# Layer A's projections by one level of Strassen's scheme, with pooled input, gate and residual kept in memory

## The chip, the cores and the metric

The kernel runs on one core of a Trainium2 chip. The metric is device time in microseconds (us); before the change the median of three runs is 2950.09 us. Engine names follow the profile: PE multiplies matrices (PEld is its weight load), DVE, ACT and POOL work elementwise, SP issues most of the DMAs. Each engine works through its own list of instructions in a fixed order; an instruction that waits holds up everything behind it on that engine.

## The reference

One step of a streaming encoder: one layer A, a shared projection to keys and values, one layer B with attention. 512 prompt positions and 8 streams of 16 new positions are worked on together: 640 columns. The change lies in layer A:

```
h = rmsnorm(x, norm_a)                        # x: 640 rows of 2048
z = h @ w_in_a                                # 2048 -> 2 * 4096
u, gate = z[..., :4096], z[..., 4096:]
# four groups g of 1024 channels, trailing windows w = 2, 4, 8, 16 along the stream
d = (windowed sum of u over w) / count - u
y = concat(d_g @ w_grp_a[g]) * scale          # 1024 -> 1024 for each group
x = x + (y * silu(gate)) @ w_out_a            # 4096 -> 2048
state = the last 15 rows of u, an output
```

After it come `hk = rmsnorm(x, norm_kv)`, `hk @ w_kv` (K, V and forget logits), layer B and the last norm. All data is float32. A product is made of three passes: each operand is split in a high part (float32r) and the rest, and high*high, high*rest and rest*high are summed.

## The kernel before

The stream lies in SBUF turned, features on partitions: `xh`, `xl` hold the two parts of the normed-by-weight input (16 k-tiles of 128 features, 640 columns), `acc` the residual. A weight tile is the stationary operand (128x128), and 320 columns of the stream pass through it; `mm3` issues the three passes for both halves, six matmuls, for a k-tile and a block of 128 outputs.

`gemm_pair` makes a pair of blocks (256 outputs). For every two k-tiles it loads 128x512 weights (`raw`), ACT writes the high part `whi`, DVE the rest `wlo`. Layer A runs by group: four `u_pair` (16 k-tiles each), then four times `gate_pair` (16 k-tiles) and `y_pair` (8 k-tiles, from the pooled input `d8`, which stays in SBUF), and `out_pairs`, the output projection over four k-tiles at a time, added to `acc` by DVE. An output bank of PSUM is one of three, so one pair can be emptied while the next is made.

`u_pair` also does the windowed sums: g + 1 additions of 774 columns for each block, on DVE (L348), then the difference `dd`. At the end of layer A `after(k)` splits each finished k-tile of `acc` and sums its squares on POOL (L473), beside the last output projections; `norm_stream` makes the row factor `R` from the sums, and `proj` starts K.

PE's order is the program's (`manual_schedule`); the order on the other engines is set by a scheduler when the kernel is built.

```
def mm3(acc_, wh, wl, xh, xl, first, last):
    for w, x, f, l in ((wh, xh, first, False), (wh, xl, False, False), (wl, xh, False, last)):
        for s in range(2):
            nc.tensor.matmul(acc_[:, s, :HALF], w, x[:, s * HALF : (s + 1) * HALF], start=f, stop=l)
```

Of the kernel before, what the change touches and what calls it, by code (L numbers as in the profile page):

```python
# [39 lines left out]
def tile_yoco_step(ctx, tc, i, o):  # L40
# [5 lines left out]
    big = ctx.enter_context(tc.tile_pool(name="big", bufs=1))  # L46
    wp = ctx.enter_context(tc.tile_pool(name="wp", bufs=1))
# [22 lines left out]
    R = const.tile([P, NT], F32, name="R")  # L70

    ps = ctx.enter_context(tc.tile_pool(name="ps", bufs=1, space=PSUM))
# [6 lines left out]

    def wchunk(src, nk, nn, scale=None, pin=False):  # L80
        raw = wp.tile([P, nk, nn], F32, tag="raw", name="raw", bufs=4)
        dma(raw, src)
        if scale is not None:
            nc.vector.tensor_tensor(raw, raw, scale.unsqueeze(2).to_broadcast([P, nk, nn]), op=ALU.mult)
        hi = wp.tile([P, nk, nn], F32R, tag="whi", name="whi", bufs=3)
        lo = wp.tile([P, nk, nn], F32R, tag="wlo", name="wlo", bufs=3)
        split(hi, lo, raw, pin)
        return hi, lo

    def mm3(acc_, wh, wl, xh, xl, first, last):  # L90
        for w, x, f, l in ((wh, xh, first, False), (wh, xl, False, False), (wl, xh, False, last)):
            for s in range(2):
                nc.tensor.matmul(acc_[:, s, :HALF], w, x[:, s * HALF : (s + 1) * HALF], start=f, stop=l)  # L93
# [18 lines left out]

    def tbank():
        return ps.tile([P, 512], F32, tag="t", name="tb", bufs=2)

    def transpose(out, x, n=P):
        nc.tensor.transpose(out, x, ident[:n, :n])  # L117
# [54 lines left out]
    win = i["w_in_a"][0].rearrange("(kt p) n -> p kt n", p=P)  # L172
    wkv = i["w_kv"].rearrange("(kt p) n -> p kt n", p=P)
    winb = i["w_in_b"][0].rearrange("(kt p) n -> p kt n", p=P)
    woutb = i["w_out_b"][0].rearrange("(kt p) n -> p kt n", p=P)
    wout = i["w_out_a"][0].rearrange("(kt p) n -> p kt n", p=P)

# [14 lines left out]

    xh = big.tile([P, KT, NT], F32R, tag="xh", name="xh")
# [4 lines left out]
    ordered = ctx.enter_context(ExitStack())  # L198
    ordered.enter_context(tc.manual_schedule(engines={mybir.EngineType.PE}))
    with tc.tile_pool(name="pa", bufs=1) as pa, tc.tile_pool(name="psa", bufs=1, space=PSUM) as psa:  # L200
        count = [0]

        def psmm():
            count[0] += 1
            if count[0] % 3 == 0:
                return psa.tile([P, 2, 512], F32, tag="mmx", name="mmx")
            return ps.tile([P, 2, 512], F32, tag="mm", name="mm", bufs=2)

        def load_rows(names, c0):
            rows = pa.tile([96, P], F32, tag="s0", name="rows")  # L210
            r0 = 0
            for nm in names:
                v = i[nm] if len(i[nm].shape) == 1 else i[nm][0]
                n = v.shape[0] // P
                dma(rows[r0 : r0 + n, :], v.rearrange("(r c) -> r c", c=P))
                r0 += n
            pc = tbank()
            transpose(pc[:, :r0], rows[:r0, :], r0)
            nc.vector.tensor_copy(cols[:, c0 : c0 + r0], pc[:, :r0])

        xq = [pa.tile([P, 4, TT, 256], F32, tag=t, name="xq") for t in ("dh", "dl")]
        ssq = pa.tile([P, TT, 2], F32, tag="mh", name="ssq", bufs=2)

        # the array's clock is raised once the array is busy: it is kept busy from the start
        idle = pa.tile([P, P], F32, tag="s1", name="idle")
        nc.vector.memset(idle, 0.0)
        warm = psa.tile([P, 2, 512], F32, tag="mmx", name="warm")
        for _ in range(8):
            nc.tensor.matmul(warm[:, 0, :P], idle, idle, start=True, stop=True)

        def load_eighth(e):
            x = xq[e // 4][:, e % 4]
            cs = slice(e * 256, (e + 1) * 256)
            if e == 0:
                load_rows(("norm_a",), 0)
            dma(x[:, 4, :], i["x_sample"].rearrange("b s d -> (b s) d")[:, cs])
            dma(x[:, :4, :], i["x_prompt"][0].rearrange("(t p) d -> p t d", p=P)[:, :, cs])

        def turn_eighth(e):
            x = xq[e // 4][:, e % 4]  # L240
            ks = slice(2 * e, 2 * e + 2)
            tp = ps.tile([P, 2, P], F32, tag="t", name="tp", bufs=2)
            for j in range(2):
                transpose(tp[:, j, :], x[:, 4, j * P : (j + 1) * P])
            xg = pa.tile([P, 2, P], F32, tag="tmp", name="xg")
            nc.vector.tensor_tensor(xg, tp, na_c[:, ks].unsqueeze(2).to_broadcast([P, 2, P]), op=ALU.mult)
            split(xh[:, ks, NP:], xl[:, ks, NP:], xg)
            nc.scalar.activation(acc[:, ks, NP:], tp, AF.Copy)
# [60 lines left out]
        def xs(k):  # L309
            return xh[:, k, :], xl[:, k, :]  # L310
# [697 lines left out]
```

## Time and profile before

| what | value |
|---|---|
| runs | 2948.26, 2950.09, 2950.49 us |
| profiled execution, first to last instruction | 2944.0 us |
| around it, against the median | 6.1 us |
| PE busy | 2921.5 us (99%) |
| DVE busy | 1457.7 us (50%) |
| ACT busy | 847.9 us (29%) |
| POOL busy | 34.7 us (1%) |
| layer A, to its last matmul | 1608 us |

How to read it: layer A takes a little over half of the span, and PE is busy throughout; the other engines have idle time. A busy PE is not a PE at its peak, since matmuls overlap, so the pace is read from the time between starts. Busy times of neighbouring DVE instructions overlap too: a 128x512 subtraction is listed with 0.68 us, and the next instruction starts 0.61 us after it.

### The profile page before, as it was taken

Reading aid. Unit: us, or ns where it says so; the run is one execution under the profiler, and the core shown is the slowest. Engines: PE = TensorE matmul, PEld = TensorE weight load, DVE = VectorE, ACT = ScalarE, POOL = GpSimd, SP = SyncE. Lnnn points to the kernel's source line nnn. Section 1 sums busy time; section 2 is a strip of 40 time slices with the busy share of each in tenths; the row PEclk is TensorE's granted clock in tenths of the full one; section 3 lists DMA queues with packets and bytes.
Section 4 is the critical chain, followed back from the end, with each engine's and each line's share of the span. In section 5 each row is a group of like instructions: output and inputs, shape, how many; then the busy total and the mean of one; then the engine's idle time right before and its main releaser. Section 6 shows DMA issues by size and latency. Waiting matters only on the chain.

```text
span 2944.0 us, 47606 instructions
## 1 busy us (share of the span) xinstructions
PE 2921.5 (99%) x19573; PEld 2828.4 (96%) x19573; DVE 1457.7 (50%) x2587; ACT 847.9 (29%) x1560; POOL 34.7 (1%) x73
## 2 busy tenths in 40 slices
PE   9999999999999999999999999999999999999998
PEld 9999999999999999999999899999999999999786
DVE  6423344333445333554337755655656666556434
ACT  5222222221222212222224232333333333334222
POOL 0000000000000000000003000000000000000000
PEclk9999999999999999999999999999999999999999
DMA  4222222222222222222224655455554555554822
GB/s 149 81 78 76 76 79 78 81 75 76 79 77 83 75 76 76 79 80 78 76 76 140 132 122 119 112 119 123 134 119 114 119 120 121 118 119 108 145 86 108
DMA packets 610282, 293.04 MB, mean 100 GB/s; under 512 B 281024, under 2 KB 595712, under 8 KB 609936
## 3 DMA queue, kind: packets, MB, share of 16 engines
q1 hardware_dynamic: 610064, 290.00, 38.5%
q8 instruction: 153, 2.51, 0.4%
q14 instruction: 65, 0.53, 0.1%
HBM read 261.28 MB, written 28.64 MB: 98 GB/s over the span
## 4 chain that ended last, share of the span: by engine, by line
PE 93%; DMA 2%; DVE 2%; SPq 1%; ACT 1%; issue 1%; DVEq 0%; POOL 0%; POOLq 0%; ACTq 0%
PE mm L93 35%; PE mmb L93 29%; PE mmx L93 17%; PE mmf L900 4%; PE po L832 2%; PE tb L117 1%; PE f L900 1%; PE ss L733 1%; DMA xt<-xres 1%; SPq L938 1%; DVE yn L941 0%; DMA raw<-in_w_in_b 0%; PE sp L743 0%; PE op L845 0%; PE op L844 0%
## 5 line engine op out<-in xcount | busy, mean ns | idle before, releaser
L78 DVE TENSOR_TENSOR wlo<-raw,whi 128x512 fp32r<-128x512 f32 x480 | 337.6, 704 | 793.6 <-ACT whi L75 791.4
L75 ACT ACTIVATE whi<-raw 128x512 fp32r<-128x512 f32 x480 | 302.7, 631 | 1012.2 <-PE mm L93 588.8
L93 PE MATMUL mmb<-xh,whi 128*128 128x320 f32 x2048 | 483.1, 317 | 2.6 <-DVE acc L413 2.6
L93 PE MATMUL mmb<-xh,wlo 128*128 128x320 f32 x2048 | 467.1, 309 | 0.0
L93 PE MATMUL mmb<-xl,whi 128*128 128x320 f32 x2048 | 466.9, 309 | 0.0
L93 PEld LDWEIGHTS mmb<-xh,whi 128*128 128x128 f32 x2048 | 337.1, 189 | 8.9 <-issue 6.5
L93 PEld LDWEIGHTS mmb<-xh,wlo 128*128 128x128 f32 x2048 | 342.9, 188 | 0.0
L93 PEld LDWEIGHTS mmb<-xl,whi 128*128 128x128 f32 x2048 | 342.8, 188 | 0.0
L93 PE MATMUL mm<-xh,whi 128*128 128x320 f32 x1408 | 325.8, 313 | 1.3 <-ACT xh L258 1.3
L93 PE MATMUL mm<-xl,whi 128*128 128x320 f32 x1408 | 321.7, 310 | 0.3 <-DVE xl L259 0.2
L93 PE MATMUL mm<-xh,wlo 128*128 128x320 f32 x1408 | 321.3, 309 | 0.0
L142 DVE TENSOR_TENSOR wlo<-raw,whi 128x512 fp32r<-128x512 f32 x272 | 188.3, 693 | 204.5 <-ACT whi L140 200.4
L140 ACT ACTIVATE whi<-raw 128x512 fp32r<-128x512 f32 x272 | 171.6, 632 | 377.4 <-PE mmb L93 232.1
L93 PEld LDWEIGHTS mm<-xl,whi 128*128 128x128 f32 x1408 | 235.6, 188 | 1.4 <-DVE xl L259 1.3
L93 PEld LDWEIGHTS mm<-xh,wlo 128*128 128x128 f32 x1408 | 235.8, 188 | 0.0
L93 PEld LDWEIGHTS mm<-xh,whi 128*128 128x128 f32 x1408 | 234.0, 188 | 1.8 <-ACT xh L258 1.5
L131 DVE TENSOR_TENSOR raw<-raw,cols 128x512 f32<-128x512 f32 x256 | 169.3, 676 | 4.8 <-DMA raw<-in_w_kv 2.2
L93 PE MATMUL mm<-mh,whi 128*128 128x320 f32 x688 | 157.4, 310 | 0.4 <-ACT whi L75 0.4
L93 PE MATMUL mm<-mh,wlo 128*128 128x320 f32 x688 | 156.7, 309 | 0.0
L93 PE MATMUL mm<-ml,whi 128*128 128x320 f32 x688 | 156.4, 308 | 0.0
L93 PE MATMUL mmx<-xh,whi 128*128 128x320 f32 x640 | 147.2, 311 | 0.0
L93 PE MATMUL mmx<-xh,wlo 128*128 128x320 f32 x640 | 145.8, 309 | 0.0
(306 smaller groups left out, 4187.9 us busy)
## 6 DMA issues: line engine op xcount, KB each, us to landing
raw<-in_w_in_a SPq DMA_DIRECT2D x256, 256.0 KB, 2.7
raw<-in_w_out_a SPq DMA_DIRECT2D x128, 256.0 KB, 2.8
raw<-in_w_kv SPq DMA_DIRECT2D x128, 256.0 KB, 3.0
raw<-in_w_in_b SPq DMA_DIRECT2D x128, 256.0 KB, 3.0
raw<-in_w_grp_a SPq DMA_DIRECT2D x64, 256.0 KB, 2.7
kc<-in_cache_k SPq DMA_DIRECT2D x64, 256.0 KB, 4.8
vc<-in_cache_v SPq DMA_DIRECT2D x16, 1024.0 KB, 7.6
raw<-in_w_out_b SPq DMA_DIRECT2D x64, 256.0 KB, 3.0
```

The source lines that it names most:

```text
L75: a = nc.scalar.activation(hi, x, AF.Copy)
L78: nc.vector.tensor_tensor(lo, x, hi.bitcast(F32), op=ALU.subtract)
L93: nc.tensor.matmul(acc_[:, s, :HALF], w, x[:, s * HALF : (s + 1) * HALF], start=f, stop=l)
L117: nc.tensor.transpose(out, x, ident[:n, :n])
L131: nc.vector.tensor_tensor(r, r, raws[n][1].unsqueeze(2).to_broadcast([P, 4, P]), op=ALU.mult)
L140: nc.scalar.activation(hi, raw, AF.Copy)
L142: nc.vector.tensor_tensor(lo, raw, hi.bitcast(F32), op=ALU.subtract)
L733: nc.tensor.matmul(sp[rows, b % 2 * PAST : (b % 2 + 1) * PAST], qs[:, rows], kct[:, b * PAST : (b + 1) * PAST], start=True, stop=True)
L832: nc.tensor.matmul(po[32 * q : 32 * q + 32, :P], pts[:, j, 32 * q : 32 * q + 32], vc[:, 4 * q + j, :], start=(j == 0), stop=False)
L900: nc.tensor.matmul(out, (ol if q == 2 else oh)[:, k, ts], wl if q == 1 else wh, start=first and q == 0, stop=last and q == 2)
L938: dma(xt[at].rearrange("p t (j r) -> p t j r", r=32), xres[n * 512 : (n + 1) * 512].rearrange("(j c) (t a r) -> a c t j r", c=32, a=4, r=3 ...
```

## The change

Layer A is written anew; K, V, layer B and the end keep their code. The matrix products of layer A go by blocks of 2x2: two k-tiles, two blocks of outputs, two halves of 320 columns. Seven products of block combinations take the place of eight products of blocks:

- `prep` makes, for two such pairs of k-tiles, the four combinations of the weights (three DVE instructions), then splits all seven operands at once (128x1792, ACT and DVE). Two buffers hold the outcome (`wh`, `wl`).
- `tbuild` makes the same for the stream side: four sums of 128x320, then split.
- `pair` runs one unit of 256 outputs: for each pair of k-tiles 7 x 3 matmuls into seven PSUM banks `m1` to `m7`, one buffer each. `combine` turns the seven banks into the four blocks (one copy on ACT, seven instructions on DVE).
- Phases: first the whole input is loaded, normed, turned and built into operands `kps` (`p0`); the turned residual goes to memory (`xacc`). Then 32 units, u and gate in turn, with the pooled input stored to memory (`dscr`) and the gate too (`gscr`). Then by group four `y_pair` and eight `out_pair`, whose outcome is added to `xacc` by an accumulating DMA from POOL's queue. At the end `acc` is loaded from `xacc`, and all 16 k-tiles are split and squared there.
- The windowed additions, and half of the sums for `kps`, go from DVE to POOL.
- Pools of later stages wait by tile.

The heart of the diff, cut:

```
+    PROD = (("m1", 1, 1), ("m6", 6, 6), ("m5", 3, 4), ("m7", 2, 5), ("m2", 5, 3), ("m3", 7, 2), ("m4", 4, 7))
...
+        def prep():
+            if raws:
+                w8 = raws.pop(0)
+                nc.vector.tensor_tensor(w8[:, :, 2:4, :], w8[:, :, 1:5:3, :], w8[:, :, 0:1, :].to_broadcast([P, 2, 2, P]),
+                                        op=ALU.subtract)
+                nc.vector.tensor_tensor(w8[:, :, 6, :], w8[:, :, 3, :], w8[:, :, 1, :], op=ALU.add)
+                nc.vector.tensor_tensor(w8[:, :, 7, :], w8[:, :, 6, :], w8[:, :, 5, :], op=ALU.subtract)
+                wh = wa.tile([P, 2, 7, P], F32R, tag="wh", name="wh", bufs=2)
+                wl = wa.tile([P, 2, 7, P], F32R, tag="wl", name="wl", bufs=2)
+                split(wh, wl, w8[:, :, 1:, :])
...
+        def pair(kps, hook=None):
+            pp = {m: psa.tile([P, 512], F32, tag=m, name=m)[:, :HALF] for m, _, _ in PROD}
+            for s in range(len(kps) // 2):
+                wh, wl = parts.pop(0)
+                prep()
+                fetch()
+                for kk in range(2):
+                    kp = 2 * s + kk
+                    h, l = kps[kp]
+                    for m, a, b in PROD:
+                        for q, (w, x) in enumerate(((wh, h), (wh, l), (wl, h))):
+                            nc.tensor.matmul(pp[m], w[:, kk, a - 1, :], x[:, b - 1, :], start=kp + q == 0,
+                                             stop=kp == len(kps) - 1 and q == 2)
...
+        def combine(pp, dst):
+            nc.scalar.activation(v, pp["m1"], AF.Copy)
+            nc.vector.tensor_tensor(u, v, pp["m6"], op=ALU.add)
+            nc.vector.tensor_tensor(e, u, pp["m5"], op=ALU.subtract)
+            put("c22", e, "m7", ALU.subtract)
+            nc.vector.tensor_tensor(u, u, pp["m7"], op=ALU.subtract)
+            put("c11", v, "m2", ALU.add)
+            put("c12", e, "m3", ALU.subtract)
+            put("c21", u, "m4", ALU.subtract)
...
+        def tbuild(x4, t, eng=None):
+            eng.tensor_tensor(t[:, 0, :], x4[:, 0, :], x4[:, 1, :], op=ALU.subtract)
+            nc.scalar.activation(h[:, 0:3, :], x4[:, 1:4, :], AF.Copy)
+            eng.tensor_tensor(t[:, 1, :], x4[:, 2, :], x4[:, 0, :], op=ALU.add)
+            eng.tensor_tensor(t[:, 2, :], x4[:, 2, :], t[:, 0, :], op=ALU.add)
+            nc.vector.tensor_tensor(l[:, 0:3, :], x4[:, 1:4, :], h[:, 0:3, :].bitcast(F32), op=ALU.subtract)
+            eng.tensor_tensor(t[:, 3, :], t[:, 2, :], x4[:, 3, :], op=ALU.subtract)
+            nc.scalar.activation(h[:, 3:7, :], t, AF.Copy)
+            nc.vector.tensor_tensor(l[:, 3:7, :], t, h[:, 3:7, :].bitcast(F32), op=ALU.subtract)
...
-                    nc.vector.tensor_tensor(nx[:, e0:], cur[:, e0:], cur[:, e0 - sh : UW - sh], op=ALU.add)
+                        nc.gpsimd.tensor_tensor(nx[:, e0:], cur[:, e0:], cur[:, e0 - sh : UW - sh], op=ALU.add)
...
+                    store(dscr[4 * g + p][b * P : (b + 1) * P, :], dd)
...
+            def out_pair(g, c, mk):
+                pp = pair(mk)
+                x4 = x4tile("o4")
+                combine(pp, into(x4))
+                nc.gpsimd.dma_start(pair_rows(xacc[c]), x4.rearrange("p (k s) n -> p k (s n)", k=2), accum_op=ALU.add)
...
+                    y_pair(g, p, dk, mk)
+                nd = []
+                if g < 3:
+                    work.append(d_side(g + 1, nd))
+                for c in range(8):
+                    out_pair(g, c, mk)
...
+    for j in range(8):
+        dma(acc[:, 2 * j : 2 * j + 2], pair_rows(xacc[j]))
+    prime()
...
+        for k in range(KT):
             split(xh[:, k, :], xl[:, k, :], acc[:, k, :])
```

`d_side` loads the pooled input of the next group and calls `tbuild` on it; it runs in pieces between the matmuls of the first output units.

How the order stands at three places. First, DVE in the last group behind a u unit. Before, the windowed additions (`sw`) stand among the weight splits (`wlo`) on DVE itself:

```order
L348 TENSOR_TENSOR sw<-ub 128x774
L78 TENSOR_TENSOR wlo<-raw,whi 128x512
L348 TENSOR_TENSOR sw<-sw 128x772
L348 TENSOR_TENSOR sw<-sw 128x768
L348 TENSOR_TENSOR sw<-sw 128x760
L351 TENSOR_TENSOR dd<-sw,inv 128x15
L353 SCALAR_TENSOR_TENSOR dd<-sw,ub 128x497
```

Now, behind `combine`, there are the weight splits (`wl`) of the gate unit that follows, and between them the differences `dd` of the two blocks, whose input `sw` comes from POOL:

```order
L73 TENSOR_TENSOR wl<-w_7083,wh 128x1792
L141 TENSOR_TENSOR w_7246<-w_7246 128x2x256
L143 TENSOR_TENSOR w_7246<-w_7246 128x2x128
L144 TENSOR_TENSOR w_7246<-w_7246 128x2x128
L367 TENSOR_TENSOR dd<-sw,inv 128x15
L369 SCALAR_TENSOR_TENSOR dd<-sw,ub 128x497
L368 TENSOR_TENSOR dd<-dd,ub 128x15
L372 SCALAR_TENSOR_TENSOR dd<-sw,ub 128x128
L141 TENSOR_TENSOR w_7297<-w_7297 128x2x256
L73 TENSOR_TENSOR wl<-w_7134,wh 128x1792
L143 TENSOR_TENSOR w_7297<-w_7297 128x2x128
L144 TENSOR_TENSOR w_7297<-w_7297 128x2x128
```

The additions left DVE, and each `dd` now stands ahead of the next weight split, with a wait for POOL in front of it.

Second, DVE in the y units. Before, a pair costs DVE two scalings and two splits between the weight splits:

```order
L401 SCALAR_TENSOR_TENSOR sg<-mmx,cols,sg 128x640
L78 TENSOR_TENSOR ml<-sg,mh 128x640
L401 SCALAR_TENSOR_TENSOR sg<-mm,cols,sg 128x640
L78 TENSOR_TENSOR wlo<-raw,whi 128x512
L78 TENSOR_TENSOR ml<-sg,mh 128x640
L78 TENSOR_TENSOR wlo<-raw,whi 128x512 x7
```

Now, from the end of `combine` of the second y unit (`cu<-cu` and the two rows after its weight split read its banks) to the start of that of the third:

```order
L187 TENSOR_TENSOR cu<-cu,m_8913 128x320
L73 TENSOR_TENSOR wl<-w_8924,wh 128x1792
L178 TENSOR_TENSOR m_9019<-ce,m_8915 128x320
...
L207 TENSOR_TENSOR tt<-m_9019 128x320
L208 TENSOR_TENSOR tt<-m_9019,tt 128x320
L209 TENSOR_TENSOR xl<-m_9019,xh 128x960
L210 TENSOR_TENSOR tt<-tt,m_9019 128x320
L141 TENSOR_TENSOR w_9060<-w_9060 128x2x256
L141 TENSOR_TENSOR w_9111<-w_9111 128x2x256
L73 TENSOR_TENSOR wl<-w_8975,wh 128x1792
L212 TENSOR_TENSOR xl<-tt,xh 128x1280
```

The split for the first step of the third unit (`wl<-w_8924`) stands inside the `combine` of the second, and that for its second step (`wl<-w_8975`) behind nearly all of `tbuild`.

Third, POOL at the end of layer A. Before, it adds squares beside the last output projections:

```order
L473 TENSOR_TENSOR sq<-sq,sqk 128x640 x15
L670 MEMSET cm 128x128
L673 MEMSET sm 128x128
L51 AFFINE_SELECT cm<-cm 128x128
L51 AFFINE_SELECT sm<-sm 128x128
```

Now the accumulating DMAs come first, and the squares only behind the last of them and some constants of layer B:

```order
L447 DMA xacc_86<-o_14975 128x2x640
L760 MEMSET cm 128x128
L763 MEMSET sm 128x128
L49 AFFINE_SELECT cm<-cm 128x128
L49 AFFINE_SELECT sm<-sm 128x128
L768 MEMSET fs 128x512
L49 AFFINE_SELECT sm<-sm 128x128
L945 MEMSET wr 128x512
L571 TENSOR_TENSOR sq<-sq,sqk 128x640
```

The constants and the squares moved behind the last transfer. `cm` lies where the sources of the accumulating DMAs lay, and waits for all of them. SP's queue reads in the same way: the eight loads of `acc`, then the first weights of K.

More of the change, by code (lines that the diff above doesn't have):

```diff
@@ L78, in split @@
         nc.vector.tensor_tensor(lo, x, hi.bitcast(F32), op=ALU.subtract)
[L80 to L93, printed above, removed]
     work = []
@@ L113, in tbank, with mm3 @@
+    def mm3(acc_, wh, wl, xh, xl, first, last):
+        for w, x, f, l in ((wh, xh, first, False), (wh, xl, False, False), (wl, xh, False, last)):
+            for s in range(2):
+                nc.tensor.matmul(acc_[:, s, :HALF], w, x[:, s * HALF : (s + 1) * HALF], start=f, stop=l)
     def tbank():
         return ps.tile([P, 512], F32, tag="t", name="tb", bufs=2)
-    def transpose(out, x, n=P):
-        nc.tensor.transpose(out, x, ident[:n, :n])
     loads, raws, parts = [], [], []
@@ L170, in proj @@
         return pp
[L172 to L176, printed above, removed]
     def queue(src, c0, scale):
```

550 lines of the change are left out of this document (287 added, 263 removed).

## The prediction

> **What bounds the kernel now.** I read the head of the page, the chain that ended last, then windows over layer A alone, and last the timelines of DVE, POOL and PE where the change sits.
>
> ```profile
> span 2944.0 us, 47606 instructions
> PE 2921.5 (99%) x19573; PEld 2828.4 (96%) x19573; DVE 1457.7 (50%) x2587; ACT 847.9 (29%) x1560; POOL 34.7 (1%) x73
> PE 93%; DMA 2%; DVE 2%; SPq 1%; ACT 1%; issue 1%; DVEq 0%; POOL 0%; POOLq 0%; ACTq 0%
> ```
>
> The chain is PE at 93%: matmuls at their pace are the time. Two windows over layer A and a piece of the chain:
>
> ```profile
> 0.00:1588.00 1588.00, 1583.33 (x10793) 1579.62 (x10794) 673.92 (x1080) 417.64 (x753) 16.67 (x46) 1.00 0.28 83
> 0.00:1610.00 1610.00, 1592.57 (x10752) 1578.42 (x10752) 1.00 0.28 83
> 179.81 28.16 PE mm L93 x192
> ```
>
> The first row (busy us and counts of PE, PEld, DVE, ACT, POOL; then granted clock, DMA share, GB/s) says that in layer A DVE works 674 of 1588 us, POOL 17, and DMA fills 0.28. The second, for the line of `mm3` alone, counts 10,752 matmuls. The chain's piece gives the pace: 28.16 / 192 = 0.1467 us.
>
> My mark is the first matmul of K, at 1610.60 us. What follows it keeps its code, and I take its time unchanged.
>
> **Matmuls.** After, each u or gate unit has 8 x 21 = 168, each y or output unit 84: 32 x 168 + 48 x 84 = 9408, 1344 fewer, worth 197 us if the pace holds. Everything below is what is given back.
>
> **Start.** Now nothing multiplies until the whole input is turned.
>
> ```profile
> 0.00:10.00 10.00, 6.93 (x30) 5.68 (x30) 3.37 (x23) 4.24 (x8) 0.70 (x6) 1.00 0.74 228
> 10.00:20.00 10.00, 10.00 (x63) 9.77 (x63) 6.88 (x13) 6.58 (x15) 0.00 (x0) 0.83 1.03 355
> ```
>
> On PE and ACT:
>
> ```profile
> 8.93 0.71 PE L93 MATMUL mm<-xh,whi 128*128 128x320 f32 x2 [1.30 <-ACT xh L258]
> 14.65 0.60 PE L117 MATMUL tpx<-ident,xq 128*128 128x128 f32 x4
> L269 ACT ACTIVATE junk<-xq 128x1024 f32<-128x1024 f32 x10 | 10.6, 1062 | 0.1
> ```
>
> Before, the first matmul started at 8.93 us. After, input and first weights, 6.2 MB, come at 228 and then 355 GB/s: about 21 us. Ten squares of 1.06 us stand ahead of the bank copies on ACT, so banks come free from 24 us on; some 132 of 160 transposes (0.15 us each, 0.60 / 4) remain, 20 us, and 5 for the waits of the last scaling: operands can be built from 50 us. For that, DVE's prices:
>
> ```profile
> 1331.06 0.68 DVE L78 TENSOR_TENSOR wlo<-raw,whi 128x512 fp32r<-128x512 f32 x1
> 1331.67 0.48 DVE L337 TENSOR_TENSOR ub<-mm,R 128x320 f32<-128x320 f32 x1
> 1332.07 0.81 DVE L78 TENSOR_TENSOR dl<-dd,dh 128x640 fp32r<-128x640 f32 x1
> 1332.80 0.35 DVE L338 TENSOR_TENSOR ub<-mm,R 128x192 f32<-128x192 f32 x1
> L401 DVE SCALAR_TENSOR_TENSOR sg<-mm,cols,sg 128x640 f32<-128x640 f32 x20 | 17.6, 881 | 7.0 <-PE mm L93 7.0
> 1327.13 2.94 DVE L348 TENSOR_TENSOR sw<-sw 128x772 f32<-128x772 f32 x3
> ```
>
> From start to start 320 columns cost 0.40 us, 512 cost 0.61, 640 cost 0.73: about 0.08 plus 1.04 ns a column. The three dependent additions of some 770 take 0.98 each against 0.88 by that line, so an instruction that needs the one before it costs 0.10 more. Hence 960 columns 1.07, 1280 1.40, 1792 1.94. One `prep` is 0.61 + 0.44 + 0.44 + 1.94 = 3.43 us of DVE, `combine` 7 x 0.41 + 0.3 = 3.2, `tbuild` 4 x 0.41 + 0.3 + 1.07 + 1.40 = 4.4. At the start DVE has eight low splits (19.8), four sets of sums (7.8) and three `prep` (10.2): 38 us, against POOL's 16 sums, 12 us by the row of 640 columns below, which partly block DVE. The first unit, 24.6 us on PE, is fed by this and ends at 50 + 38 + up to 12, plus 3 for its last matmuls: between 85 (half the transposes hidden) and 105; I take 98.
>
> The other 9240 matmuls take 1355 us, 68 transposes of states and pool rows 10. With 27 for the end of layer A (below): 98 + 1355 + 10 + 27 = 1490, which is 120 us ahead of the mark.
>
> **u and gate units.** DVE has 2 x (4 x 3.43 + 3.2) = 34 us of work in 49 us of PE, and only waits can hurt: `dd` stands ahead of the next weight split and needs POOL.
>
> ```profile
> L473 POOL TENSOR_TENSOR sq<-sq,sqk x15: 1558/1594/1869, 1561.7 to 1614.9; 128x640 f32<-128x640 f32 x15
> 1597.85 1.73 POOL L473 TENSOR_TENSOR sq<-sq,sqk 128x640 f32<-128x640 f32 x1 [0.85 <-ACT sqk L472]
> ```
>
> and on DVE in the same microseconds:
>
> ```profile
> 1598.07 2.19 DVE L78 TENSOR_TENSOR xl<-acc,xh 128x640 fp32r<-128x640 f32 x1
> 1600.18 0.68 DVE L78 TENSOR_TENSOR wlo<-raw,whi 128x512 fp32r<-128x512 f32 x1
> 1600.78 0.81 DVE L413 TENSOR_TENSOR acc<-mm,acc 128x640 f32<-128x640 f32 x1
> 1602.40 0.83 DVE L78 TENSOR_TENSOR xl<-acc,xh 128x640 fp32r<-128x640 f32 x1 [0.81 <-ACT xh L75]
> ```
>
> A POOL addition of 640 columns takes 1.59 us, so one of 774 some 1.9, twice DVE's. And the split at 1598.07, beside the addition of 1597.85 to 1599.58, took 2.19 us where the one at 1602.40 took 0.83: it stood still for 1.4 of the 1.73. In group 3 the chain after a u unit is eight additions, 15 us; `dd` of the second block waits for all of it, and the split for the third step of the gate unit stands behind, while PE has 2 x 6.2 us of steps in hand. Walking through the row of instructions gives PE waits, for groups 0 to 3, of 0, 0, 0.7 and 6 us a pair of units if POOL and DVE don't hinder each other, and 0, 2.8, 6.7 and 11 if they block fully; times four, 27 and 82. Since 1.4 of 1.73 was blocked, but `combine` reads PSUM and another part of DVE's work falls outside the additions, I take 66.
>
> The Trainium skill, "SBUF — State Buffer", section "SBUF: two separate sides", calls this port an exclusive lock, where the loser blocks for the whole instruction. By that the term is 82 and the sum 16 us more; the row, with 1.4 us of 1.73, stands just below it.
>
> **y and output units.** PE needs 84 x 0.1467 = 12.3 us a unit. DVE needs in a y unit two `prep` 6.9, `combine` 3.2, two scalings 1.6 (0.88 busy, 0.81 apart), `tbuild` 4.4: 16.1. In an output unit 10.1, and in the first two of a group four `tbuild` more (17.6). With two buffers of split weights DVE can't run ahead, so it bounds y units and the first two output units: 4 x 16.1 + 2 x 10.1 + 17.6 = 102 against 6 x 12.3 = 74. That floor is 28 us for each of groups 0 to 2 and 16 for the last, 100 in all. Walking through the order, where the first split of a unit stands inside the `combine` of the one before, gives units of 12.3, 16.4, 18.3, 20.4, 18.8 and 24.2, 36 us over PE, and 145 in all at the high end. I take 36 x 3 + 22 = 130: the order repeats and gives no reason to reach the floor. The first four `tbuild` of group 0 stand ahead of the first y unit, with its data loaded only then: 8 more (0 to 15).
>
> **DMA.** Pooled input, gate and residual add some 40 MB in layer A, 25 GB/s on 83, where the start showed 355: hidden. Stores wait on SP behind their source; the weight loads behind them are three buffers (18 us) ahead.
>
> **End of layer A.** K's operands now come by way of memory.
>
> ```profile
> xres<-acc SPq DMA_DIRECT2D x4, 1280.0 KB, 5.2
> xt<-xres SPq DMA_DIRECT2D x16, 320.0 KB, 6.9
> out_pool_sample<-po SPq DMA_DIRECT2D x32, 60.0 KB, 2.0
> L472 ACT ACTIVATE sqk<-acc 128x640 f32<-128x640 f32 x15 | 11.0, 734 | 0.4 <-POOL sq L473 0.4
> 1607.52 0.45 PE L93 MATMUL mm<-mh,wlo 128*128 128x320 f32 x2
> 1610.60 0.53 PE L93 MATMUL mmb<-xh,whi 128*128 128x320 f32 x2 [2.63 <-DVE acc L413]
> ```
>
> Before, 2.6 us lay between the two products. After: `combine`'s last block 1.4 us after the last matmul; the accumulating DMA, which no row shows, 2 to 10 by these three (I take 6, nearest `xt<-xres`, of the same 320 KB); the load of `acc` behind it on SP as much or less, with the weights for K in the queue behind it; ACT copies and squares in turn, 0.74 each, and its squares have two buffers that POOL empties at 1.6 us, behind 1.4 us of constants. ACT's first weight split stands behind the twelfth square: 7.4 + 1.4 + some 11 x 1.6 = 26. So K starts 27 us later, range 15 to 35.
>
> The Trainium skill, "DMA: Bandwidth & Descriptors", section "Anatomy of one DMA — SWDGE (gpsimd) path", fits such a transfer by 2.0 us plus its bytes over 436e3: an estimate of 2.8 us for 327,680 bytes, and a sum 3 us smaller. No run here shows it.
>
> **Sum.** -120 + 66 + 130 + 8 = +84 us on the span: 3028. Around the span lie 6.1 us to the median (2950.1 - 2944.0): 3034 us, 2.8% slower.
>
> **Rivals.** (1) Faster: DVE keeps up, since the scheduler's order lets it fill waits that my walk counts. It decides where the three stall terms (66, 130, 8) are together under 120. The floors 27 + 100 + 0 = 127, with the start at 85 and the end at 15, give -18: 2932. For more, DVE's long splits must be cheaper than the line says (no row goes beyond 774 columns): at 1.75 us instead of 1.94 a y unit falls to 15.6 and the floor of 100 to some 85: 2917. Range 2850 to 2944; against it stands that the rows of 320 to 772 columns lie on the line. (2) No change: stalls at their floors, the lock without effect, start and end nearly as taken: -120 + 127 = +7, 2944 to 2956. That needs the scheduler to hit every floor. (3) Much slower: stalls cost clock too.
>
> ```profile
> 1610.60 8.53 PE mmb L93 x46
> 1611.00:1612.00 1.00, 1.00 (x6) 1.00 (x6) 0.73 (x1) 1.00 (x3) 0.00 (x0) 0.59 0.49 148
> ...
> 1613.00:1614.00 1.00, 1.00 (x6) 1.00 (x5) 1.00 (x1) 0.60 (x1) 1.00 (x1) 0.50 0.24 97
> ```
>
> After the idle 2.63 us the granted clock was 0.59 and 0.50, and 46 matmuls took 8.53 us instead of 6.75: 1.8 lost. If each of some 20 stalls above 2.6 us costs that, +36: 3070; with the walk and the lock at their high ends (+15, +16), 3101. An accumulating DMA that lands after more than 22 us would also hold the output units (two `o4` buffers), and each us above that adds up to 16.
>
> The Trainium skill, "TensorE: Matmul & The Clock Gate", section "What's actually happening", puts the drop behind an idle window of some 3.4 us; the row shows one behind 2.63, so the measurement decides.
>
> **How the numbers follow.** About 6 us (0.2%) is what a measurement can tell from no change. My forecast, DVE-bound y units and POOL-fed waits at 2956 to 3060, has 0.58; rival 1 0.17; rival 2 0.05; rival 3 0.20. Slower is 0.78. The range 2915 to 3125 leaves about 0.1 on each side.
>
> **What would show it.** 9408 matmuls, close to 0.147 us apart inside a unit; DVE at 1270 us of work in layer A and near full in y units, where PE waits for DVE's `wl` and `combine`; in groups 2 and 3 `dd` waiting for POOL's `sw`, and weight splits longer beside it; the first unit done at 98 us; a gap of 27 us before K, with POOL's squares back to back. I am wrong if PE stays above 97% between 100 us and K, or if the matmuls themselves run slower than 0.147 with new shapes of operands.

## The result and the profile after

The changed kernel takes 3105.8 us (median of four), the kernel before 2949.2 in the same series: a ratio of 1.054, 95% interval 1.052 to 1.056. It is 5.4% slower where 2.8% was forecast. One execution of e4 below took 15,383 us, five times its others, and is left out of its median. From the page of the changed kernel:

```profile
span 3105.6 us, 45691 instructions
PE 2850.5 (92%) x18299; PEld 2703.6 (87%) x18299; DVE 2057.3 (66%) x3478; ACT 1017.0 (33%) x1418; POOL 254.3 (8%) x201
```

A window over layer A, for the line of its matmuls:

```profile
0.00:1760.00 1760.00, 1505.57 (x9408) 1444.49 (x9408) 0.94 0.40 116
```

The 9408 matmuls are there, and 600 us more of DVE. PE's share fell from 99% to 92%, and the granted clock over layer A (third column from the end of the window) from 1.00 to 0.94.

ACT copies the bank `m1` once in each unit (`cv`), when PE is some 2.6 us from the unit's end; from one copy to the next is one unit. The tile's view:

```profile
L183 ACT ACTIVATE cv<-m x80: 416/438/447, 107.7 to 1729.1; 128x320 f32<-128x320 f32 x80
```

Three rows of PE's timeline:

```profile
106.20 0.66 PE L94 MATMUL tb<-ident,st 120*128 120x120 f32 x2 [6.90 <-DMA st<-in_state_pool]
1731.34 0.31 PE L166 MATMUL m<-xh,wl 128*128 128x320 f32 x1
1770.37 0.90 PE L482 MATMUL mmb<-xh,whi 128*128 128x320 f32 x2 [38.72 <-ACT whi L508]
```

The last row is K's first matmul, at 1770.4 instead of 1610.6: layer A lost 159.8 us, and what follows 2 more. Windows from the first `cv` to that of the last gate unit, and from there to the last `cv`:

```profile
107.71:965.18 857.47, 810.27 (x5290) 793.73 (x5290) 596.57 (x882) 276.87 (x321) 160.31 (x110) 0.97 0.34 108
965.18:1729.09 763.91, 659.20 (x4020) 624.16 (x4019) 597.10 (x923) 248.31 (x205) 37.89 (x31) 0.94 0.45 117
```

At 0.1467 us a matmul the 31 units of the first row need 764 us, and 10 for transposes: 84 are lost. The 48 y and output units need 591: 173 are lost. The second pair of numbers, the time in which weights are loaded, splits these losses: loads run back to back while matmuls do, so what lies above 774 and 591 is matmuls at a lower clock (20 and 33 us), and the rest, 64 and 140 us, is PE standing still. This split is an estimate to some 5 us: half of the time in which weights were loaded at a granted clock of 0.50 is 23 and 38 us.

Whom PE waited for, the first row in the u and gate units, the others in the y and output units (us in total, times, longest):

```profile
PE m L166 <- DVE wl L73: 36.9, 23, 4.3
...
PE m L166 <- DVE cu L187: 56.4, 38, 6.3
PE m L166 <- DVE cu L184: 13.8, 28, 1.9
```

In u and gate units it is the weight split `wl`; in y and output units `combine`, which frees the banks. All waits listed for PE add up to 47 and 103 us, less than 64 and 140: a matmul is listed as busy for 0.31 us where the pace is 0.147, which hides the first part of each wait.

### The profile page after: what moved, and what is told of

Read it like the earlier page. It is cut to its first block, busy times and chain, and to the rows that moved or that the text cites. A ratio compares the mean times of both kernels' runs of the same rounds, so it can differ in the third digit from the quotient of the medians.

```text
span 3105.6 us, 45691 instructions
## 1 busy us (share of the span) xinstructions
PE 2850.5 (92%) x18299; PEld 2703.6 (87%) x18299; DVE 2057.3 (66%) x3478; ACT 1017.0 (33%) x1418; POOL 254.3 (8%) x201
## 4 chain that ended last, share of the span: by engine, by line
PE 47%; DVE 9%; DMA 6%; issue 3%; ACT 1%; SPq 1%; POOL 1%; DVEq 0%; ACTq 0%; POOLq 0%
PE mmb L482 29%; PE m L166 7%; PE mmf L990 4%; DVE wl L73 3%; DMA w<-in_w_out_a 2%; DMA w<-in_w_grp_a 2%; PE po L922 2%; PE ss L823 1%; DMA xt<-xacc 1%; PE f L990 1%; PE tb L94 1%; DVE o L178 1%; ACT wh L70 1%; SPq L1028 1%; DVE w L141 1%
## 5 line engine op out<-in xcount | busy, mean ns | idle before, releaser
L166 PE MATMUL m<-xh,wh 128*128 128x320 f32 x3136 | 1019.7, 325 | 109.4 <-DVE cu L187 60.3
L166 PE MATMUL m<-xh,wl 128*128 128x320 f32 x3136 | 999.9, 319 | 45.5 <-DVE wl L73 45.1
L166 PE MATMUL m<-xl,wh 128*128 128x320 f32 x3136 | 997.4, 318 | 11.8 <-DVE xl L212 8.4
L166 PEld LDWEIGHTS m<-xh,wh 128*128 128x128 f32 x3136 | 613.2, 196 | 149.3 <-DVE cu L187 75.8
L166 PEld LDWEIGHTS m<-xh,wl 128*128 128x128 f32 x3136 | 613.4, 196 | 57.0 <-DVE wl L73 56.5
L166 PEld LDWEIGHTS m<-xl,wh 128*128 128x128 f32 x3136 | 614.2, 196 | 14.4 <-DVE xl L212 10.7
L70 ACT ACTIVATE wh<-w 128x1792 fp32r<-128x1792 f32 x224 | 380.8, 1700 | 663.5 <-PE m L166 532.9
L482 PE MATMUL mmb<-xh,whi 128*128 128x320 f32 x2048 | 483.8, 317 | 38.7 <-ACT whi L508 38.7
L73 DVE TENSOR_TENSOR wl<-w,wh 128x1792 fp32r<-128x1792 f32 x224 | 461.1, 2058 | 72.7 <-ACT wh L70 72.4
L510 DVE TENSOR_TENSOR wlo<-raw,whi 128x512 fp32r<-128x512 f32 x272 | 187.4, 690 | 199.5 <-ACT whi L508 195.8
L508 ACT ACTIVATE whi<-raw 128x512 fp32r<-128x512 f32 x272 | 171.6, 632 | 386.0 <-PE mmb L482 227.7
```

Of the source, the lines that this page charges most:

```text
L70: a = nc.scalar.activation(hi, x, AF.Copy)
L73: nc.vector.tensor_tensor(lo, x, hi.bitcast(F32), op=ALU.subtract)
L166: nc.tensor.matmul(pp[m], w[:, kk, a - 1, :], x[:, b - 1, :], start=kp + q == 0, stop=kp == len(kps) - 1 and q == 2)
L508: nc.scalar.activation(hi, raw, AF.Copy)
L510: nc.vector.tensor_tensor(lo, raw, hi.bitcast(F32), op=ALU.subtract)
```

## The experiments

All numbers below are of one profiled execution each, beside the median of the runs. "u, gate" and "y, out" are the two stretches above, "to K" the time from the last `cv` to K's first matmul. Kernels that share the code of a stretch differ there by up to 10 us (853 to 863 in the first), so smaller differences are not read.

| kernel | median us | ratio to before (95%) | first `cv` | u, gate | y, out | to K |
|---|---|---|---|---|---|---|
| the change | 3105.8 | 1.054 (1.052-1.056) | 107.7 | 857.5 | 763.9 | 41.3 |
| e1 additions on DVE | 3041.1 | 1.032 (1.031-1.034) | 107.3 | 789.9 | 762.6 | 41.1 |
| e9 no wait for POOL | 3113.2 | 1.056 (1.055-1.058) | 109.6 | 863.5 | 761.7 | 40.8 |
| e3 plain store | 3056.3 | 1.037 (1.036-1.039) | 107.5 | 858.1 | 714.0 | 39.8 |
| e10 no low parts | 3019.1 | 1.024 (1.022-1.026) | 109.1 | 852.9 | 690.5 | 37.9 |
| e4 builds spread | 3086.2 | 1.047 (1.045-1.049) | | | | |
| e7 written order | 3077.6 | 1.044 (1.043-1.046) | 110.1 | 806.1 | 784.2 | 41.5 |
| e12 filler | 3103.1 | 1.053 (1.051-1.055) | 107.8 | 863.4 | 749.6 | 41.1 |
| e11 sums at start | 3102.9 | 1.053 (1.051-1.055) | 101.2 | 859.5 | 764.9 | 41.3 |
| e5 squares on DVE | 3094.2 | 1.050 (1.048-1.052) | 107.9 | 857.6 | 761.3 | 29.9 |
| e8 written, K early | 3056.9 | 1.037 (1.036-1.039) | 108.6 | 806.2 | 780.8 | 7.8 |
| e6 e1 + e4 + e5 | 3021.0 | 1.025 (1.024-1.027) | 109.3 | 791.6 | 748.0 | 29.4 |
| e13 e1 + e11 + e12 + end | 3011.5 | 1.022 (1.021-1.024) | 101.0 | 795.4 | 754.0 | 7.8 |

**POOL in the u and gate units.** e1:

```diff
-  nc.gpsimd.tensor_tensor(nx[:, e0:], cur[:, e0:], cur[:, e0 - sh : UW - sh], op=ALU.add)
+  nc.vector.tensor_tensor(nx[:, e0:], cur[:, e0:], cur[:, e0 - sh : UW - sh], op=ALU.add)
```

> The windowed additions go back from POOL to DVE, all else as in the changed kernel. Theory (POOL's long additions and the port they share with DVE hold back the weight splits of the gate unit behind a u unit): the units behind a u unit, which took 25.6, 26.3, 29.6 and 32.8 us on average in groups 0 to 3 against 24.6 us of matmuls, come down to 25 to 27 us; about 50 us off the time (40 to 65), 3040 to 3065 us. Rival (DVE itself has no room for eight additions of 0.98 us between the splits of group 3, so the wait only changes its name): group 3 stays above 30 us, less than 20 us off.

Measured: 65 us off, all of it in this stretch. The units behind a u unit went from 25.9, 26.3, 29.6 and 32.9 us to 25.4, 24.9, 24.8 and 25.2, and the clock of the stretch from 0.97 to 1.00. The rival is out, but for a small part: with the additions on DVE the u units of group 3 rose from some 25.4 to 27.5 us. Which of POOL's two effects it was, e9 tells: there every addition and `dd` read `ub`, so DVE waits for POOL no more.

```diff
-  nx = pu.tile([P, UW], F32, tag=f"s{lv % 2}", name="sw")
+  nx = pu.tile([P, UW], F32, tag="s0", name="sw")
-  cur, sh = nx, sh * 2
+  sh = sh * 2
-  dd = pu.tile([P, NT], F32, tag=f"s{(g + 1) % 2}", name="dd")
+  dd = pu.tile([P, NT], F32, tag="s1", name="dd")
```

> The windowed additions stay on POOL in number and size, but each reads the u block itself, and the differences on DVE are taken from the u block, so the sums over the window are left out: DVE no longer waits for POOL, while both still use the port. Theory A (the wait in DVE's order is what costs: the difference stands ahead of the next weight split): the units behind a u unit fall to 25 to 27 us in all groups, 40 to 60 us off the time of the changed kernel, nearly as much as the 65 us that additions on DVE saved. Theory B (the port: every POOL addition stops DVE's splits for most of its time): group 3 stays above 29 us, less than 20 us off.

Measured: nothing gained; the units of group 3 still take 32.9 us. Theory A is out, and the traces show the port at work. In the changed kernel, DVE behind a u unit of group 3, then POOL:

```profile
853.04 1.96 DVE L141 TENSOR_TENSOR w<-w 128x512 f32<-128x512 f32 x1
855.03 1.58 DVE L143 TENSOR_TENSOR w<-w 128x256 f32<-128x256 f32 x1
856.65 1.57 DVE L144 TENSOR_TENSOR w<-w 128x256 f32<-128x256 f32 x1
859.96 0.17 DVE L367 TENSOR_TENSOR dd<-sw,inv 128x15 f32<-128x15 f32 x1 [1.73 <-POOL sw L364]
...
870.31 0.17 DVE L367 TENSOR_TENSOR dd<-sw,inv 128x15 f32<-128x15 f32 x1 [4.82 <-POOL sw L364]
...
854.53 5.39 POOL L364 TENSOR_TENSOR sw<-sw 128x772 f32<-128x772 f32 x3
```

In e9 the same place, without the waits:

```profile
802.79 1.45 DVE L367 TENSOR_TENSOR dd<-ub,inv 128x15 f32<-128x15 f32 x1
804.75 1.44 DVE L368 TENSOR_TENSOR dd<-dd,ub 128x15 f32<-128x15 f32 x1
806.32 1.95 DVE L141 TENSOR_TENSOR w<-w 128x512 f32<-128x512 f32 x1
808.30 1.95 DVE L143 TENSOR_TENSOR w<-w 128x256 f32<-128x256 f32 x1
801.08 10.50 POOL L364 TENSOR_TENSOR sw<-ub 128x774 f32<-128x774 f32 x5 [39.21 <-ACT last L359]
```

Beside POOL's chain a TENSOR_TENSOR of DVE with two inputs in SBUF takes about as long as an addition of POOL: 1.95 us for 256 columns that else take 0.42, 1.45 for 15 columns that else take 0.17. In e9 DVE gets five of them in beside the five additions of the row, whatever their size. The SCALAR_TENSOR_TENSOR among them (`dd<-ub`, 497 columns), which reads `ub` twice, took 0.66 us, no longer than elsewhere. The long TENSOR_TENSORs agree with the exclusive lock of the Trainium skill, "SBUF — State Buffer", section "SBUF: two separate sides". Where `dd` waits, DVE loses that time to the wait; where it doesn't, to the port.

**The accumulating transfer.** e3:

```diff
-  nc.gpsimd.dma_start(pair_rows(xacc[c]), x4.rearrange("p (k s) n -> p k (s n)", k=2), accum_op=ALU.add)
+  nc.gpsimd.dma_start(pair_rows(xacc[c]), x4.rearrange("p (k s) n -> p k (s n)", k=2))
```

> The transfer of an output unit overwrites the residual in memory instead of adding to it, so the sum over groups and the input are left out; same bytes written, nothing read and added. Theory A (the accumulating transfer, 6.5 us long, sits in the DMA engines ahead of the next weight load, so the load lands 6 us after its issue instead of 3.5, DVE waits for it with the ready weight split and combine queued behind, and PE waits for its banks): output units 4 to 8 of a group fall from 14.2 us on average to 12.5 to 13, 25 to 40 us off in all. Theory B (the order on DVE alone: the next combinations stand ahead of a ready split, and the load cannot come earlier because its buffer is free late): no more than 8 us off. Under both the gap ahead of K may shrink by 2 to 5 us.

Measured: 50 us off, all in the y and output units; outputs 4 to 8 of a group went from 14.2 to 12.3 to 12.6. How DVE goes through an output unit of the changed kernel:

```profile
1688.29 0.69 DVE L141 TENSOR_TENSOR w<-w 128x512 f32<-128x512 f32 x1 [5.00 <-DMA w<-in_w_out_a]
1688.89 2.02 DVE L73 TENSOR_TENSOR wl<-w,wh 128x1792 fp32r<-128x1792 f32 x1
1690.83 0.42 DVE L143 TENSOR_TENSOR w<-w 128x256 f32<-128x256 f32 x1
1691.16 0.48 DVE L184 TENSOR_TENSOR cu<-cv,m 128x320 f32<-128x320 f32 x1
...
1687.83 0.44 ACT L183 ACTIVATE cv<-m 128x320 f32<-128x320 f32 x1 [1.97 <-PE m L166]
```

DVE stands 5 us for a weight load. Behind it wait the split `wl` and behind that `combine`, whose first sum could have started at 1688.3, with ACT's copy, and started 2.9 us later; PE runs into full banks. The transfer (size, us to landing) in the change, then in e3:

```profile
xacc<-o POOLq DMA_DIRECT2D x32, 640.0 KB, 6.5
```

```profile
xacc<-o POOLq DMA_DIRECT2D x8, 640.0 KB, 3.5
```

The weight load for which DVE stands above, issued 2.2 us after such a transfer:

```profile
w<-in_w_out_a SPq DMA_DIRECT2D x1, 512.0 KB, 5.7
```

Of the 64 loads of `in_w_out_a` 13 are issued while a transfer runs; they land after 5.8 us in the median, the others after 3.5. In e3 it is 3.6 and 3.5.

DVE's waits for weights in the y and output units, the change first:

```profile
DVE w L141 <- DMA w<-in_w_out_a: 67.4, 15, 5.9
DVE w L141 <- DMA w<-in_w_grp_a: 47.1, 9, 7.2
```

```profile
DVE w L141 <- DMA w<-in_w_out_a: 38.9, 15, 4.3
DVE w L141 <- DMA w<-in_w_grp_a: 25.6, 9, 4.3
```

Adding in memory takes 6.5 us where a store takes 3.5, and DVE's waits for weights fall by 50 us with it. (By the Trainium skill, "DMA: Bandwidth & Descriptors", section "Anatomy of one DMA — SWDGE (gpsimd) path", 655,360 bytes are an estimated 3.5 us: the plain store agrees, the adding one doesn't.) So theory A holds, but not alone: e7 keeps the transfer and changes the order on DVE.

```diff
+  sa.enter_context(tc.manual_schedule(engines={mybir.EngineType.DVE}))
...
-                prep()
-                fetch()
+                sums()
...
+                if s < len(kps) // 2 - 1:
+                    parted()
+                    fetch()
...
             put("c21", u, "m4", ALU.subtract)
+            parted()
+            fetch()
```

(`sums` and `parted` are the two halves of `prep`; the additions of the windows come one at a time through `work`.)

> DVE runs the units in an order written out: a unit's banks are combined as soon as they are full, then the ready weight split, then the next weight combinations; the windowed additions are on DVE, one at a time between the k-tile pairs of the following unit, the builds for the next group spread over eight output units. The gap ahead of K is left as it is, and so is the accumulating transfer. Theory (order on DVE turns a late load or a long split into a wait of PE for its single-buffered banks; DVE's sum is left as the only bound): u and gate units 24.7 to 25.5 us, y units some 16 us, output units 12.3 to 13, time 2930 to 2965 us. Rival (the accumulating transfer delays the weight loads whatever the order): output units stay at 14, time 2985 to 3010 us.

Measured: 28 us off, far from the forecast. What it was right in: units behind a u unit take 24.6 us, the pace of the matmuls; and the last six output units of group 3, with the accumulating transfer in place, go at the pace too:

```profile
1626.35 0.44 ACT L196 ACTIVATE cv<-m 128x320 f32<-128x320 f32 x1 [1.92 <-PE m L176]
1638.77 0.44 ACT L196 ACTIVATE cv<-m 128x320 f32<-128x320 f32 x1 [1.98 <-PE m L176]
1651.11 0.44 ACT L196 ACTIVATE cv<-m 128x320 f32<-128x320 f32 x1 [1.98 <-PE m L176]
```

A weight load behind such a transfer is as late there, and DVE's only waits in these units are for ACT:

```profile
w<-in_w_out_a SPq DMA_DIRECT2D x1, 512.0 KB, 6.1
```

```profile
DVE wl L73 <- ACT wh L70: 15.1, 6, 4.2
```

So the late load alone doesn't cost PE; it does in the order of the change, where a split that is ready stands behind it. (The written order also issues the loads at another place; this run doesn't part the two.) What the forecast was wrong in: in group 3 the additions only moved the wait to the u units (29.7 us), most y units took 18 to 21 us (the first 31.9), the first two output units of a group 18 to 20, and later ones with a build 15 to 17, since in this order DVE waits for ACT inside a build and ahead of a split:

```profile
1586.17 1.49 DVE L227 TENSOR_TENSOR xl<-tt,xh 128x1280 fp32r<-128x1280 f32 x1 [1.34 <-ACT xh L226]
...
1590.99 2.03 DVE L73 TENSOR_TENSOR wl<-w,wh 128x1792 fp32r<-128x1792 f32 x1 [1.81 <-ACT wh L70]
```

The period of 19.1 us (from the split at 1571.90 to that at 1590.99) less these waits is 15.9 us of DVE work, where the prediction's prices gave 16.1.

**DVE's sum.** e10:

```diff
-  l = xtile([P, 7, HALF], F32R, "xl")
+  l = xtile([P, 7, HALF], F32R, "xl") if low else h
...
-  nc.vector.tensor_tensor(l[:, 3:7, :], t, h[:, 3:7, :].bitcast(F32), op=ALU.subtract)
+  if low:
+      nc.vector.tensor_tensor(l[:, 3:7, :], t, h[:, 3:7, :].bitcast(F32), op=ALU.subtract)
```

> In the y and output units the low parts of the stream operands are left out (two DVE subtractions of 960 and 1280 columns for each of 32 builds; the high part is multiplied in their place, so matmuls are as many). Theory (DVE's sum bounds y units and the first two output units): DVE's work for a y unit falls from 16.1 to 13.6 us and the four builds beside the output units from 17.6 to 7.7, so 20 us less in groups 0 to 2 and 10 in the last, 70 us in all, 3025 to 3050 us. Rival (late weight loads, banks and the order hold PE there, not DVE's sum): less than 30 us off, above 3075.

Measured: 73 us off in the y and output units, 87 in the median. The y units fell from 15.8 to 14.1 us on average, and outputs 1 to 3 of the four groups from 225 to 172 us together, so the rival is out there: DVE's work is what bounds them. Outputs 4 to 8, from which no work was taken, stayed at 14.1 to 14.9, as the rival has it. In e3, where the transfer no longer disturbs, PE stands still 97 us by the same split as above (714.0 less 591, less 25 at a lower clock); the floor of the prediction was 100. That all of the 97 is DVE's sum isn't shown, since DVE still waits 64 us for weights there.

e4 moves the builds for the next group:

```diff
-                    yield
+                    for _ in range(4):
+                        yield
                     out.append(tbuild(x4, ttile()))
-                    yield
+                    for _ in range(4):
+                        yield
```

> The four stream-side builds for the next group are spread over all eight output units of groups 0 to 2 instead of the first two; same instructions. Theory (DVE's sum bounds the y units and the first two output units): outputs 1 to 3 fall from 58 us together to some 46, outputs 4 to 8 rise by 0.5 to 1 us each since DVE then has 12.3 us of work in each of them; 15 to 30 us off in all. Rival 1 (output units are held by weight loads and banks, not by DVE's sum): outputs 4 to 8 stay at 14.2, 35 us off or more. Rival 2 (every build held back behind a late load costs a whole wait): no gain.

Measured: 20 us off by the median, 22 by the ratio, as the theory had it. Its units are read in e6, which holds the same edit beside e1 and e5.

> Three edits at once: windowed additions on DVE, builds for the next group spread over eight output units, squares ahead of K on DVE. If the three hit separate waits, their gains (65, 20 and 12 us) add up: 3005 to 3015 us. If the spread builds only shift DVE's load to the output units that wait for late weight loads, outputs 4 to 8 go to 15 us and above, and the sum is 10 to 20 us short of that.

Measured: 3021 us, some 10 us short of the sum. In groups 0 to 2 outputs 1 to 3 fell from 59.6 to 46.5 us together, but outputs 4 to 8 rose from 14.3 to 15.8, one of them to 21 or 22: the second case of the expectation.

**The clock.** PE's wait in a y unit of the changed kernel:

```profile
1219.19 0.42 PE L166 MATMUL m<-xh,wh 128*128 128x320 f32 x1 [3.23 <-DVE cu L187]
```

Windows of 1 us behind it:

```profile
1220.00:1221.00 1.00, 1.00 (x5) 1.00 (x5) 1.00 (x2) 0.00 (x0) 0.00 (x0) 0.50 1.03 355
1222.00:1223.00 1.00, 1.00 (x6) 1.00 (x5) 1.00 (x4) 0.56 (x1) 0.00 (x0) 0.50 0.34 44
1223.00:1224.00 1.00, 1.00 (x8) 1.00 (x8) 1.00 (x2) 0.00 (x0) 0.00 (x0) 0.93 0.76 289
```

After 3.23 us of standing still the clock is 0.50 for over 3 us, which costs an estimated 1.6 to 1.7. e12 puts work into that wait:

```diff
+                        if fill and kp == 0 and m == "m7":
+                            tb = tbank()
+                            for _ in range(fill):
+                                nc.tensor.matmul(tb[:, :P], ident, ident, start=True, stop=True)
...
-                pp = pair(dk)
+                pp = pair(dk, fill=8)
...
-                pp = pair(mk)
+                pp = pair(mk, fill=8 if c < 2 else 0)
```

> Eight small matmuls (128x128, into the spare bank, read by nobody) stand in PE's order ahead of the product that waits for the bank of m7, in the 16 y units and the first two output units of each group: about 1.2 us of work inside a wait that was 3.2 us long, after which the granted clock was 0.50 for 3.4 us. Theory (the clock drops because PE stands still that long; 2 us of standing still in the later output units did not drop it): the drops of these units go, 1.6 us each, 15 to 30 us off in all. Rival (the clock follows the mean load of the unit, or the filler pushes later work back): no gain, or 5 to 25 us more.

Measured: a unit of the change from `cv` to `cv`, PE's wait in e12 (the profile lists the eight small matmuls as 16), and two like units of e12:

```profile
1212.10:1229.45 17.35, 14.12 (x86) 13.86 (x85) 15.59 (x24) 6.13 (x5) 0.00 (x0) 0.90 0.30 98
```

```profile
1213.74 1.95 PE L168 MATMUL tb<-ident 128*128 128x128 f32 x16
1216.62 0.41 PE L170 MATMUL m<-xh,wh 128*128 128x320 f32 x1 [0.94 <-DVE cu L191]
```

```profile
1209.93:1225.34 15.41, 14.47 (x102) 14.18 (x101) 14.91 (x23) 6.01 (x5) 0.00 (x0) 1.00 0.33 112
1225.34:1240.12 14.78, 14.38 (x102) 13.90 (x100) 14.46 (x24) 6.90 (x7) 0.00 (x0) 1.00 0.37 116
```

The wait is 0.94 us instead of 3.23, the clock 1.00 instead of 0.90, and the unit 2 us shorter although PE does more; DVE, 14.9 of 15.4 us busy, is then what bounds it. The drop is gone, as the theory had it at this place. But the busy share of PE in the unit rose too, from 0.81 to 0.94, so the run doesn't tell the length of the wait from the load. e7 does: the clock of its y and output units is 0.90, the lowest of all, though only four waits of PE there are over 2 us. Two waits and the clock behind them:

```profile
1591.01 0.41 PE L176 MATMUL m<-xh,wh 128*128 128x320 f32 x1 [1.50 <-ACT wh L70]
1593.07 0.63 PE L176 MATMUL m<-xh,wl 128*128 128x320 f32 x1 [1.50 <-DVE wl L73]
```

```profile
1596.00:1597.00 1.00, 1.00 (x5) 0.98 (x5) 1.00 (x4) 0.41 (x1) 0.00 (x0) 0.50 0.00 0
```

Two waits of 1.50 us with two matmuls between them did what one of 3.23 did. So the length of one wait isn't the measure; how little PE works over some 3 us is nearer to it, and with that to the rival. Over the stretch e12 gained 14 us, just under what was expected; in the median, 3 us against intervals of 6, it isn't resolved.

The Trainium skill, "TensorE: Matmul & The Clock Gate", section "What's actually happening", has the drop behind an idle window of about 3.4 us: here 3.23 did it, before the change 2.63, in e7 two of 1.50 close together, and 0.94 didn't, so a shorter stop is enough.

**Start and end.** e11:

```diff
-  kps.append(tbuild(x4s[j], tt, nc.gpsimd if j % 2 else None))
+  kps.append(tbuild(x4s[j], tt))
```

> At the start all sums for the stream operands are on DVE (half of them were on POOL). Theory (POOL's four sums take 4.5 us and more where DVE needs 1.9, DVE waits for them in its order, and DVE's subtractions stop beside them): the first unit ends 5 to 12 us earlier. Rival (the first unit's end is held by the late load of the pool states, for which PE waited 6.9 us ahead of its last matmuls): 0 to 4 us off.

Measured: the first `cv` 6.5 us earlier; of the time, 3 us, which the intervals don't resolve. PE still waits 6.0 us there for the load of the pool states, which comes earlier too. e5 moves the squares, and e8 adds to e7 the same edit and the weights for K ahead of `acc`:

```diff
-                nc.gpsimd.tensor_tensor(sq, sq, s, op=ALU.add)
+                nc.vector.tensor_tensor(sq, sq, s, op=ALU.add)
```

> The squares ahead of K are added on DVE instead of POOL. Theory (POOL's additions, 1.95 us each there, hold ACT's squares, two buffers, and with them ACT's first weight split behind the twelfth square): the gap between the last output matmul and K's first falls from 39 to 26 to 30 us, 9 to 13 us off. Rival (DVE, with 16 stream splits, 4 scalings and the weight splits there, becomes the bound in turn): 0 to 5 us off.

```diff
+    prime()
     for j in range(8):
         dma(acc[:, 2 * j : 2 * j + 2], pair_rows(xacc[j]))
-    prime()
```

> The written order of the run before, and at the end of layer A the weights for K loaded ahead of the residual and the squares added on DVE. Theory: the gap ahead of K falls from 39 to 18 to 28 us, so 10 to 20 us less than the run before, 2915 to 2950 us: about the time of the kernel before the change. Rival (the last accumulating transfer, 10 us, and ACT's 32 copies and squares set the gap): 5 to 10 us less.

POOL's squares in the change and its wait ahead of them, then K's first matmul in e5 and in e8:

```profile
L571 POOL TENSOR_TENSOR sq<-sq,sqk x15: 1521/1915/2012, 1746.9 to 1777.5; 128x640 f32<-128x640 f32 x15
```

```profile
1743.74 0.20 POOL L760 MEMSET cm<- 128x128 f32 x1 [9.30 <-DMA xacc<-o]
```

```profile
1756.66 0.90 PE L482 MATMUL mmb<-xh,whi 128*128 128x320 f32 x2 [27.35 <-ACT whi L508]
```

```profile
1703.38 0.90 PE L505 MATMUL mmb<-xh,whi 128*128 128x320 f32 x2 [5.18 <-ACT xh L70]
```

The squares on DVE took 11 us off the wait of 38.7, and 11.6 off the time. With the weights early the wait is 5.2 us, but the first product of K then waits step by step for `xl`: from K's first matmul to the end e8 needs 1348.7 us, the change 1335.2. Of 33 us, 21 reached the time beside e7; the rival's 5 to 10 were too few. The 2915 to 2950 us of the forecast were missed with e7's.

> Together: windowed additions on DVE (65 us), squares ahead of K on DVE and the weights for K loaded ahead of the residual (26 us in the runs in written order), sums at the start on DVE (5), and the filler (15 to 30). If these are separate waits: 2980 to 3000 us, still above the 2948 of the kernel before; if the filler costs: 3010 to 3030.

Measured: 3011.5 us, the time of the second case, but not for its reason: the filler didn't cost, it brought 9 us in its stretch, within what like kernels differ by. What fell short is the filler, with 3 us instead of 15 to 30 in e12's median, and the end, where 26 were taken and e8 had brought 21. This kernel and e6 are the fastest that compute the whole, and they are 2.2 and 2.5% slower than the kernel before the change. No version here beats it.

## Why the prediction was right in its direction, and short by 72 us

By its terms, against the 159.8 us at K's first matmul, of which it had 84 (on the span it was 78 us short; the time around the span, 1.7 us instead of 6.1, and the profiled execution, 1.5 us above the median, make that 72):

- **Matmuls**: 9408, at 0.1467 us inside a unit. Right.
- **Start**: first unit done at 98; it was 110 (the first `cv` at 107.7 and 18 matmuls more): 12 short. PE waited 6.9 us there for the load of the pool states, which the prediction left out. That sums on POOL hold DVE up was in it, and e11's 6.5 us are of that.
- **u and gate units**: 66 taken, 84 measured. The 66 were meant as standing still behind u units, and PE stood still 64; but only 44 of that in units behind a u unit, and 20 in the u units themselves, which the walk had at nothing. That the size agrees is in part luck. By e1 POOL's additions are worth 48 of the 64. The other 20 are the clock. Of the two causes given, port and wait, e9 shows that the port alone is enough.
- **y and output units**: 130 + 8 taken, 173 measured, 140 without the clock. The size of the standing still is right by luck, for its parts are not. Without the adding transfer 97 are left (e3), near the floor of 100. In place of the 38 that the walk added there are 43 us that go with the late weight loads behind the transfer, most of them in output units 4 to 8, which the prediction had at 12.3 us. "DMA ... hidden" is the step that failed: bytes over bandwidth say nothing about a load that lands 2 us late in front of a split that is ready. The landing of 22 us from which the prediction saw harm was the wrong mechanism (the two `o4` buffers); 6.5 us did harm to the weight loads issued while the transfer ran.
- **Clock**: nothing in the sum, a rival with 36 us; it cost an estimated 53. The row that priced it (1.8 us for a wait of 2.63) fits the 1.6 to 1.7 of the change, so 53 us are some 30 drops where it had 20. This and the late loads are the two terms that were missing; a sum with rival 3 in it would have been 3070.
- **End**: 27 taken for the place of K, 38.7 measured. The transfer took 9.9 us from its issue at 1733.2 to the first instruction that waited for it, at 1743.1, not 6: the prediction had 327,680 bytes, and a transfer holds two k-tiles of them. POOL's additions took 1.92 us in the median, not 1.6, and the constants ahead of them 3.2 (1743.7 to 1746.9), not 1.4; 3.5 us more of constants stood between the first three squares, which the walk didn't have.

12 + 18 + 35 + 12 = 77, rounded: the 76 us that were missing at that mark.

The rival of the other sign, DVE keeping up, needed the three stall terms under 120 us; they came to 256.

## What to carry to other kernels

Fewer matmuls are worth their time only as far as the other engines can feed the faster pace: add up DVE's work by stage, not by kernel, and compare it with PE's new time of that stage. An engine that works through its list in order passes on every wait of its own: look at what stands behind an instruction that waits for a load, and put what is ready ahead of it. Count stalls twice where they are long, or close enough together, to lower the clock, and give POOL no long operations on SBUF beside the DVE work that PE waits for: DVE was busy 597 of 857 us in the u and gate units, and still POOL's additions cost 65 us.

## What the runs showed of the hardware

- A DVE TENSOR_TENSOR of 15 columns took 1.45 us instead of 0.17 beside POOL's additions, one of 256 columns 1.95 instead of 0.42: what counts is the number of instructions that meet, not their size. A SCALAR_TENSOR_TENSOR there, which reads one tile twice, kept its 0.66 us.
- A transfer of 640 KB that adds in memory took 6.5 us to land, the same as a plain store 3.5; weight loads issued while it ran landed after 5.8 us instead of 3.5.
- A wait of 3.23 us lowered the granted clock to 0.50 for over 3 us; a like unit with the wait cut to 0.94 us by idle matmuls kept it at 1.00. Two waits of 1.50 us close together lowered it as well.
